# A scan's second try over a chunk: both chunks of a step at once, and the next step's exponents right behind the products

## The chip, the cores and the metric

The kernel runs on one core of a Trainium2 chip. The metric is device time in microseconds for one launch of the whole program (two layers). The engines are named as in the profile: PE is TensorE (matmuls; PEld is its weight load), DVE is VectorE, ACT is ScalarE, POOL is GpSimd, SP is SyncE, which issues most DMAs. PSUM is the matmuls' output memory, eight banks of 512 float32 columns for 128 partitions.

## The reference, cut to what matters

Each layer has three parallel groups of heads: a bidirectional Mamba-2 scan (SSD), windowed attention, and a convolution module. The change touches the scan alone. For each chunk of 128 tokens, each of 16 heads and each direction it computes (cut):

```python
cs = cumsum(da)                                   # inside the chunk
decay = exp(where(tril, cs[l] - cs[s], -inf))     # 128 x 128 per head
cb = einsum('lgn,sgn->gls', c, b)                 # one per group of 8 heads
y_diag = einsum('grls,sgrp->lgrp', cb * decay, x * dt)
states = einsum('lgn,grl,lgrp->grpn', b, exp(cs[-1] - cs), x * dt)
y_off = einsum('lgn,grpn,grl->lgrp', c, entering_state, exp(cs))
y = y_diag + y_off                                # forward and backward, summed
```

There are 1280 tokens, 2 chunks of context and 8 of latents, so 10 chunks. The backward direction has the mirrored mask. The forward and the backward weights of one chunk use the same `cb`, so both directions' `decay * dt` can be added before one product with `x`.

## The kernel before, in words

Each layer runs `ssd_section`, `att_section` and `out_section`, one after the other. `ssd_section` makes the scan's set-up (cumulative sums, logarithms of `dt`, and from both the tiles `L`), then for i = 0 to 3 calls `half(i, xk)` (four heads each), the gemms and taps of one convolution block (`conv_gemm(i)`, `taps()`), and `inputs(i + 1)`, the projections for the next half. `half` stands under `high_priority(AHEAD)`. The order on each engine is not the program's: a planner simulates the program at compile time, starts what is ready by priority, and takes tile slots from each tag's pool as they come free. What it decides is fixed in the program; on the chip each engine runs its instructions in that order.

A half has ten steps `(cf, cb)`: forward chunk `cf` and backward chunk `cb`. Each step multiplies the entering state (`yo`), makes the next state (`stp`, then `S`), and visits both chunks. A chunk is visited twice, once per direction. The first visit starts `yp`, the chunk's sum. The second visit (step 1 and steps 6 to 9; in the last layer steps 6 to 9 alone), called the second try here, adds `yo` and then finishes the chunk:

- `diag(c)` (L872 to L895) builds exponents on PE. The weights operand is `lt`, a tile `L`, with 99 rows used: 48 rows with the high, middle and low bfloat16 part of the negated sums for 16 (direction, head) pairs, 48 for the logarithms, 3 rows of -1. The moving operand is R, whose 96 upper rows select heads and whose rows 96 to 98 hold the chunk's sums, fetched from DRAM (`csd`) by two DMAs on ACT's queue.
- One matmul 128 wide, two of 64, and two that add a mask, go to a PSUM tile `pc`; four of 64, two of them masks, to `pd`. ACT takes the exponential of both (L884, L891), POOL adds the 64 x 64 blocks on the diagonal (L893), and DVE multiplies by `cbs` (L895).
- Two transposes of `yp` (L912) and four products with `xk` (64 wide, two passes each, so x8 in the trace) go to one PSUM tile; ACT copies it to `yT` (L916) and a DMA stores it.

So per half 10 second tries in layer 0 and 8 in layer 1, 72 in all. The tags `ex`, `eb`, `yT` and R have two buffers; the PSUM tag `sm` has four banks (NSM), which all of this, `yo`, `stp` and the transposes of `inputs` share. The gemms use two other banks (`pj`). At each half's start two DVE copies fill both R (L852).

All matmuls but the transposes go through the helper at L96, so they are told apart by tile names. The trace's form `128*64` means 128 rows and 64 columns of weights.

Of the kernel before, what the change touches and what calls it, by code (L numbers as in the profile page):

```python
# [10 lines left out]
F32 = mybir.dt.float32  # L11
# [8 lines left out]
P = 128  # L20
# [39 lines left out]
NSM = 4  # L60
# [7 lines left out]
def build(tc, A, out, stop=None, dbg=None):  # L68
# [26 lines left out]
    def mm(o, l, r, start=True, stop=True):  # L95
        nc.tensor.matmul(o, l, r, start=start, stop=stop)  # L96
# [24 lines left out]
    sel_c = cp.tile([P, 16], BF16, name="sel_c")  # L121
    sel4 = cp.tile([P, 32], F32, name="sel4")
    nc.vector.tensor_reduce(out=sel4[:, 0:16], in_=ident[:, 0:96].rearrange("p (a b) -> p b a", b=16), axis=mybir.AxisListType.X, op=ALU.add)
    nc.vector.tensor_copy(out=sel_c, in_=sel4[:, 0:16])
# [14 lines left out]
    csd = [dp.tile([2, 3, 2, 2, 4, T], BF16, name=f"cs{l}") for l in range(DEPTH)]  # L139
# [401 lines left out]
    def ssd_section(l, last, early):  # L541
        v1 = vec1[l]
        gblocks = LATB if last else ALLB
        with ExitStack() as st:
# [191 lines left out]

            nc.vector.tensor_scalar_mul(out=cs, in0=cs, scalar1=-1.0)
            L = []
            for g in range(2):
                qq = sp.tile([P, NCH, P], BF16, tag=("cbs", "btok")[g], name="qq")  # L740

                def v4(ap):
                    return ap.rearrange("p c (d j) -> p c d j", d=2)

                for c0, t in ((0, cs), (48, ld)):
                    x = v4(v3(t))[:, :, :, 8 * g:8 * g + 8]
                    q = [v4(qq[:, :, c0 + 16 * k:c0 + 16 * k + 16]) for k in range(3)]
                    nc.vector.tensor_copy(out=q[0], in_=x)
                    nc.vector.tensor_tensor(out=x, in0=x, in1=q[0], op=ALU.subtract)
                    nc.vector.tensor_copy(out=q[1], in_=x)  # L750
                    nc.vector.tensor_tensor(out=q[2], in0=x, in1=q[1], op=ALU.subtract)
                nc.gpsimd.memset(qq[:, :, 96:P], -1.0)
                lt = sp.tile([P, T], BF16, tag=f"L{g}", name="L")
                for b0 in range(0, NCH, 4):
                    nb = min(4, NCH - b0)
                    pr = pp.tile([P, 1024], BF16, tag="sm", name="pr", bufs=NSM)
                    for c in range(b0, b0 + nb):
                        nc.tensor.transpose(pr[:, (c - b0) * P:(c - b0 + 1) * P], qq[:, c, :], identb)
# [82 lines left out]
            def half(i, xk):  # L841
# [5 lines left out]
                def sel4(t):  # L847
                    return t.rearrange("p (d h) -> p d h", d=2)[:, :, 4 * hf:4 * hf + 4]
                Rs = []
                for _ in range(2):  # L850
                    R = sp.tile([P, 2, 4, P], BF16, tag="R", name="R", bufs=2)
                    nc.vector.tensor_copy(out=R, in_=sel4(sel_c).unsqueeze(3).to_broadcast([P, 2, 4, P]))  # L852
                    Rs.append(R)
# [11 lines left out]
                nv = [0]  # L865

                def diag(c):

                    R = Rs[nv[0] % 2]
                    nv[0] += 1  # L870
                    for dd in range(2):
                        nc.scalar.dma_start(out=R[96:99, dd], in_=csd[l][g, :, dd, hf, :, c * P:(c + 1) * P])  # L872

                    ll = [lt[0:99, c * P + a:c * P + a + 64] for a in (0, 64)]
                    qs = [slice(0, 64), slice(64, P)]
                    r0, r1 = R[0:99, 0], R[0:99, 1]
                    pc = pp.tile([P, 4, P], F32, tag="sm", name="pc", bufs=NSM)
                    mm(pc[:, :, qs[1]], lt[0:99, c * P:(c + 1) * P], r0[:, :, qs[1]], start=True, stop=False)
                    mm(pc[qs[0], :, qs[0]], ll[0], r0[:, :, qs[0]], start=False, stop=False)
                    mm(pc[qs[1], :, qs[0]], ll[1], r1[:, :, qs[0]], start=False, stop=False)  # L880
                    for q in qs:
                        mm(pc[q, :, q], identb[:, q], mask_lt[:, q].unsqueeze(1).to_broadcast([P, 4, 64]), start=False, stop=True)
                    e = sp.tile([P, 4, P], F32, tag="ex", name="ex", bufs=2)
                    nc.scalar.activation(out=flat(e), in_=flat(pc), func=AF.Exp)  # L884
                    pc = pp.tile([P, 4, P], F32, tag="sm", name="pd", bufs=NSM)[:, :, 0:64]
                    for q, lq in zip(qs, ll):
                        mm(pc[q], lq, r1[:, :, q], start=True, stop=False)
                    for q in qs:
                        mm(pc[q], identb[:, q], mask_gt[:, q].unsqueeze(1).to_broadcast([P, 4, 64]), start=False, stop=True)
                    eb = sp.tile([P, 4, 64], F32, tag="eb", name="eb", bufs=2)  # L890
# [579 lines left out]
```

## Time and profile before

| | us |
|---|---|
| median of 3 runs (2412.1 to 2414.97) | 2413.73 |
| the profiled execution | 2409.47 |
| its span, first to last instruction | 2407.7 |
| PE busy | 2307.0 |
| DVE busy | 1533.2 |
| POOL busy | 1085.7 |
| ACT busy | 979.0 |

The busy time of an engine is the union of its instructions' times. Matmuls are pipelined: each is shown with its whole latency, so they overlap and PE seems busy in gaps shorter than that. The distance between the starts of two matmuls, their pitch, is what one costs. Mean granted clock of TensorE over the span is 0.985 of full speed.

### The profile page before, as it was taken

What the parts mean: (1) busy time and instruction counts of PE and PEld (TensorE: products, weight loads), DVE (VectorE), ACT (ScalarE), POOL (GpSimd) and SP (SyncE); (2) the same over time, 40 slices, a digit from 0 to 9 for tenths busy, and PEclk for the clock granted to TensorE, in tenths of its full rate; (3) what the DMA queues carried; (4) which work ended last, traced back from release to release, by engine and by line L of the source; (5) the groups of instructions that cost most, each with busy time, mean ns of one, the idle gap of its engine ahead of it and who ended that gap; (6) DMA issues with size and microseconds to landing.
All of it is one profiled execution on the core that took longest, in us unless ns stands there. A gap on an engine that the chain in (4) does not pass through costs nothing.

```text
span 2407.7 us, 37133 instructions
## 1 busy us (share of the span) xinstructions
PE 2307.0 (96%) x13453; PEld 1817.5 (75%) x13453; DVE 1533.2 (64%) x2738; ACT 979.0 (41%) x2123; POOL 1085.7 (45%) x1249
## 2 busy tenths in 40 slices
PE   6999999999999999999999999999999999999998
PEld 3787678777877776776888788768768676776798
DVE  4679899941276855865354679979423864865634
ACT  6543243422235454444243443343322355463433
POOL 3237663764453222343233337667575531332333
PEclk8999999999999999999999999999999999999999
DMA  7412212233133112248465311111212312235663
GB/s 225 154 58 87 87 49 64 85 100 111 36 90 105 62 38 70 80 141 264 136 185 168 92 40 45 41 41 43 78 54 62 106 48 67 80 97 171 197 179 107
DMA packets 324248, 237.07 MB, mean 98 GB/s; under 512 B 56066, under 2 KB 280546, under 8 KB 324064
## 3 DMA queue, kind: packets, MB, share of 16 engines
q1 hardware_dynamic: 280832, 193.28, 27.2%
q10 hardware_dynamic: 42336, 41.06, 5.5%
q8 instruction: 106, 1.74, 0.3%
q0 software_dynamic: 896, 0.35, 0.1%
q14 instruction: 78, 0.64, 0.1%
HBM read 181.63 MB, written 53.00 MB: 97 GB/s over the span
## 4 chain that ended last, share of the span: by engine, by line
PE 77%; DVE 9%; DMA 5%; POOL 3%; issue 2%; ACT 2%; SPq 1%; ACTq 0%; DVEq 0%; POOLq 0%
PE pj L96 53%; PE sm L96 6%; PE s L96 4%; PE o L96 3%; PE pt L1086 3%; PE po L96 2%; DVE us L508 2%; DMA raw<-oT 1%; PE pc L96 1%; PE pm L96 1%; DMA wm<-w_mod 1%; POOL ex L893 1%; PE rb L96 1%; DVE acc L596 1%; PE sm L912 1%
## 5 line engine op out<-in xcount | busy, mean ns | idle before, releaser
L96 PE MATMUL pj<-hh,wh 128*128 128x512 f32 (+1 forms) x1840 | 692.7, 377 | 7.8 <-ACT wh L416 2.3
L96 PE MATMUL pj<-hl,wh 128*128 128x512 f32 (+1 forms) x1840 | 686.5, 373 | 1.7 <-POOL hl L199 1.7
L96 PE MATMUL pj<-hh,wl 128*128 128x512 f32 (+1 forms) x1840 | 686.4, 373 | 1.7 <-POOL wl L418 1.6
L418 POOL TENSOR_TENSOR wl<-wr,wh 128x512 fp32r<-128x512 f32 x268 | 362.1, 1354 | 516.8 <-ACT wh L416 482.1
L96 PEld LDWEIGHTS pj<-hh,wh 128*128 128x128 f32 x1840 | 350.0, 190 | 70.7 <-issue 6.8
L96 PEld LDWEIGHTS pj<-hh,wl 128*128 128x128 f32 x1840 | 349.5, 190 | 61.3 <-issue 5.0
L96 PEld LDWEIGHTS pj<-hl,wh 128*128 128x128 f32 x1840 | 350.2, 190 | 59.3 <-issue 5.7
L416 ACT ACTIVATE wh<-wr 128x512 fp32r<-128x512 f32 x344 | 215.6, 630 | 365.5 <-PE pj L96 280.2
L508 DVE SCALAR_TENSOR_TENSOR ua<-gl,vec,ua 128x512 f32<-128x512 f32 (+1 forms) x435 | 303.5, 698 | 12.3 <-ACT ua L506 5.7
L596 DVE SCALAR_TENSOR_TENSOR acc<-raw,vec,acc 128x514 f32<-128x514 f32 (+2 forms) x280 | 191.0, 695 | 21.9 <-ACT acc L593 20.3
L96 PE MATMUL pj<-ho,wh 128*128 128x256 f32 (+1 forms) x896 | 180.3, 300 | 1.0 <-ACT wh L416 1.0
L96 PE MATMUL pj<-hx,wh 128*128 128x512 f32 x512 | 163.7, 400 | 6.9 <-DVE hx L500 2.9
L96 PEld LDWEIGHTS pj<-ho,wh 128*128 128x128 f32 x896 | 145.2, 193 | 6.4 <-ACT wh L416 1.2
L893 POOL TENSOR_TENSOR ex<-ex,eb 64x256 f32<-64x256 f32 x144 | 115.5, 802 | 59.4 <-ACT eb L891 52.4
L933 POOL TENSOR_TENSOR xs<-xk,ws 128x256 f32<-128x256 f32 x144 | 90.7, 641 | 112.0 <-PE sm L96 96.8
L1079 ACT ACTIVATE p<-s,sums 128x512 f32<-128x512 f32 (+1 forms) x144 | 95.5, 663 | 107.7 <-DVE sums L1077 69.4
L1076 DVE TENSOR_REDUCE mx<-s 128x1 f32<-128x512 f32 (+1 forms) x144 | 92.4, 654 | 72.0 <-PE s L96 71.6
L96 PE MATMUL pj<-ho,wl 128*128 128x256 f32 (+1 forms) x448 | 134.6, 301 | 1.1 <-POOL wl L418 0.8
L508 DVE SCALAR_TENSOR_TENSOR us<-gl,vec,us 128x512 f32<-128x512 f32 (+1 forms) x150 | 130.3, 869 | 6.8 <-ACT us L506 4.3
L96 PEld LDWEIGHTS pj<-hx,wh 128*128 128x128 f32 x512 | 97.8, 192 | 30.6 <-DVE hx L500 4.7
L907 POOL TENSOR_TENSOR yp<-yp,ye 128x256 f32<-128x256 f32 x136 | 104.3, 783 | 26.6 <-DVE ye L906 26.1
L1086 PE MATMUL pt<-ident,p 128*128 128x128 f32 x640 | 108.5, 283 | 7.2 <-ACT p L1079 6.5
(325 smaller groups left out, 3951.6 us busy)
## 6 DMA issues: line engine op xcount, KB each, us to landing
wr<-w_in SPq DMA_DIRECT2D x160, 256.0 KB
wr<-w_out SPq DMA_DIRECT2D x114, 256.0 KB
wm<-w_mod SPq DMA_DIRECT2D x64, 256.0 KB
raw<-oT ACTq DMA_DIRECT2D x64, 256.0 KB
wr<-w_out SPq DMA_DIRECT2D x76, 128.0 KB
yT<-yT ACTq DMA_DIRECT2D x72, 128.0 KB
wm<-w_mod SPq DMA_DIRECT2D x16, 512.0 KB
wr<-w_in SPq DMA_DIRECT2D x64, 128.0 KB
```

Of the source, the lines that this page charges most:

```text
L96: nc.tensor.matmul(o, l, r, start=start, stop=stop)
L416: nc.scalar.activation(out=hi, in_=raw, func=AF.Copy)
L418: low_eng[0].tensor_tensor(out=lo, in0=raw, in1=f32(hi), op=ALU.subtract)
L508: nc.vector.scalar_tensor_tensor(out=u if t == 30 else acc, in0=g[:, t:t + n], scalar=vec2[l][:, t, j:j + 1], in1=acc, op0=ALU.mult, op1=A ...
L596: nc.vector.scalar_tensor_tensor(out=acc, in0=raw[:, i0 + t:i0 + t + n], scalar=v1[:, cw:cw + 1], in1=acc, op0=ALU.mult, op1=ALU.add)
L893: nc.gpsimd.tensor_tensor(out=e[q, :, q], in0=e[q, :, q], in1=eb[q], op=ALU.add)
L907: nc.gpsimd.tensor_tensor(out=y, in0=y, in1=ye, op=ALU.add)
L912: nc.tensor.matmul(ps[:, jj * P:(jj + 1) * P], y[:, jj * P:(jj + 1) * P], ident, start=(jj == 0), stop=False, is_transpose=True)
L933: nc.gpsimd.tensor_tensor(out=h3(xs), in0=xc(c), in1=hb(ws3, c, d), op=ALU.mult)
L1076: nc.vector.tensor_reduce(out=mx, in_=s, axis=mybir.AxisListType.X, op=ALU.min)
L1079: nc.scalar.activation(out=flat(p[:, 0:min(nk, 4), :]), in_=s, func=AF.Exp, scale=-1.0, bias=nm[:, j:j + 1], accum_out=sums[:, 3, j:j + 1])
L1086: nc.tensor.transpose(pt[:, q * P:(q + 1) * P], pr[q][:, i, :], ident)
```

## The change

`mm` returns its instruction; `after` makes the instructions traced inside it queue behind a given one on its engine. `diag` and the end of `visit` become `weights(cc)` and `outputs(cc, e)`, each for both chunks of a step. `weights` for the next second try is issued behind the last product of this one; the first is issued at the half's start. `L` now has in its lower 64 rows a 64 x 64 identity (`id64`), and R has masks there, written once per layer, so that the masks come with the same matmul. R has three variants (forward, mixed, backward) of 512 columns. `ex`, `eb` and `yT` hold two chunks and have one buffer each. R's upper rows are filled on ACT at each half's start.

```diff
-    csd = [dp.tile([2, 3, 2, 2, 4, T], BF16, name=f"cs{l}") for l in range(DEPTH)]
+    csd = [dp.tile([2, 3, 2, 3, 4, T], BF16, name=f"cs{l}") for l in range(DEPTH)]
...
+    def after(ins):
+        return tc.issue_after(ins[0].ins) if ins else nullcontext()
...
             for g in range(2):
+                qc = sp.tile([P, NCH, 72], BF16, tag="xk", name="qc", bufs=7)
+                parts(cs, qc, g)
+                for q, c0 in ((slice(0, 64), 24), (slice(64, P), 0)):
+                    nc.scalar.activation(out=qc[q, :, 48:72], in_=qc[q, :, c0:c0 + 24], func=AF.Copy)
...
+                parts(ld, qq, g)
+                nc.gpsimd.memset(qq[:, :, 48:64], -1.0)
+                nc.scalar.activation(out=qq[:, :, 64:P], in_=id64.unsqueeze(1).to_broadcast([P, NCH, 64]), func=AF.Copy)
...
+                        nc.tensor.transpose(pr[0:72, (c - b0) * P:(c - b0 + 1) * P], qc[:, c, :], identb)
+                    cr = sp.tile([72, 512], BF16, tag="xk", name="cr", bufs=7)
+                    nc.scalar.activation(out=cr[:, 0:nb * P], in_=pr[0:72, 0:nb * P], func=AF.Copy)
+                    for v, w in enumerate((0, 2, 1)):
+                        nc.scalar.dma_start(out=csd[l][g][:, :, v].rearrange("a f h t -> (a f) h t")[:, :, b0 * P:(b0 + nb) * P], in_=cr[24 * w:24 * w + 24, 0:nb * P])
...
-                nc.scalar.dma_start(out=csd[l][g].rearrange("a d f h t -> (a d f h) t"), in_=lt[0:48, :])
...
+            Rs = []
+            for _ in range(2):
+                R = sp.tile([P, 3, 4, P], BF16, tag="R", name="R", bufs=2)
+                nc.gpsimd.memset(R[32:64], 0.0)
+                nc.gpsimd.memset(R[64:P, 0:2], 0.0)
+                for v, t0, m in ((0, 0, mask_lt), (1, 64, mask_lt), (2, 0, mask_gt), (2, 64, mask_gt)):
+                    nc.gpsimd.tensor_copy(out=R[64:P, v, :, t0:t0 + 64], in_=m[64:P, 64:P].unsqueeze(1).to_broadcast([64, 4, 64]))
+                Rs.append(R)
...
-                    nc.vector.tensor_copy(out=R, in_=sel4(sel_c).unsqueeze(3).to_broadcast([P, 2, 4, P]))
+                for R in Rs:
+                    for v, d, t0, t1 in ((0, 0, 0, P), (2, 1, 0, P), (1, 1, 0, 64), (1, 0, 64, P)):
+                        nc.scalar.activation(out=R[0:48, v, :, t0:t1], in_=sel_c[0:48, d, 4 * hf:4 * hf + 4].unsqueeze(2).to_broadcast([48, 4, t1 - t0]), func=AF.Copy)
...
+                def weights(cc):
+                    pcs = []
+                    pd = pp.tile([P, 2, 4, 64], F32, tag="sm", name="pd", bufs=NSM)
+                    e = sp.tile([P, 2, 4, P], F32, tag="ex", name="ex")
+                    eb = sp.tile([P, 2, 4, 64], F32, tag="eb", name="eb")
+                    for R, c in zip(Rs, cc):
+                        nc.scalar.dma_start(out=R[48:51], in_=csd[l][g, :, hf, :, :, c * P:(c + 1) * P])
+                    with after(last_mm):
+                        for u, (R, c) in enumerate(zip(Rs, cc)):
+                            ll = [lt[:, c * P + a:c * P + a + 64] for a in (0, 64)]
+                            pc = pp.tile([P, 4, P], F32, tag="sm", name="pc", bufs=NSM)
+                            for v, (q, lq) in enumerate(zip(qs, ll)):
+                                mm(pc[q], lq, R[:, v])
+                            for q, lq in zip(qs, ll):
+                                mm(pd[q, u], lq, R[:, 2, :, q])
+                            pcs.append(pc)
+                    for u in range(2):
+                        nc.scalar.activation(out=flat(e[:, u]), in_=flat(pcs[u]), func=AF.Exp)
+                    nc.scalar.activation(out=eb, in_=pd, func=AF.Exp)
+                    for q in qs:
+                        nc.gpsimd.tensor_tensor(out=e[q, :, :, q], in0=e[q, :, :, q], in1=eb[q], op=ALU.add)
+                    for u, c in enumerate(cc):
+                        nc.vector.tensor_tensor(out=e[:, u], in0=e[:, u], in1=cbs[:, c, :].unsqueeze(1).to_broadcast([P, 4, P]), op=ALU.mult)
+                    return e
...
+                def outputs(cc, e):
+                    ps = sm()
+                    for u, c in enumerate(cc):
+                        for jj in range(2):
+                            nc.tensor.matmul(ps[:, (2 * u + jj) * P:(2 * u + jj + 1) * P], yp[c // 2][:, c % 2, jj * P:(jj + 1) * P], ident, start=(u + jj == 0), stop=False, is_transpose=True)
+                    for u, c in enumerate(cc):
+                        for h in range(4):
+                            k = 2 * u + h // 2
+                            last_mm[:] = [mm(ps[h % 2 * 64:h % 2 * 64 + 64, k * P:(k + 1) * P], xk[c // 2][:, c % 2, h * 64:(h + 1) * 64], e[:, u, h, :], start=False, stop=(u * 2 + h // 2 == 3))]
+                    yT = sp.tile([P, 4, P], F32, tag="yT", name="yT")
+                    nc.scalar.activation(out=flat(yT), in_=ps, func=AF.Copy, scale=0.5)
+                    for u, c in enumerate(cc):
+                        nc.scalar.dma_start(out=yTd[l][:, 2 * i:2 * i + 2, c * P:(c + 1) * P], in_=yT[:, 2 * u:2 * u + 2, :])
...
+                second = ([] if last else [1]) + [6, 7, 8, 9]
+                e = weights(steps[second[0]])
...
+                        if si in second:
+                            outputs((cf, cb), e)
+                            if si < 9:
+                                e = weights(steps[second[second.index(si) + 1]])
```

## Rows read from the trace of the kernel before

**Rows 1.** The page: engine sums (busy us, share, instructions), and the chain by engine.
```profile
PE 2307.0 (96%) x13453; PEld 1817.5 (75%) x13453; DVE 1533.2 (64%) x2738; ACT 979.0 (41%) x2123; POOL 1085.7 (45%) x1249
...
PE 77%; DVE 9%; DMA 5%; POOL 3%; issue 2%; ACT 2%; SPq 1%; ACTq 0%; DVEq 0%; POOLq 0%
```

**Rows 2.** Busy us by stage (a:b, length, then each engine; last clock and DMA).
```profile
core 0: us, PE busy (x) PEld busy (x) DVE busy (x) ACT busy (x) POOL busy (x), PEclk, DMA share, GB/s
...
160.00:500.00 340.00, 331.48 (x2115) 256.07 (x2114) 307.18 (x531) 123.69 (x265) 216.87 (x320) 1.00 0.26 75
500.00:620.00 120.00, 113.34 (x685) 86.43 (x684) 33.78 (x64) 32.59 (x67) 66.59 (x85) 0.97 0.33 93
1400.00:1700.00 300.00, 291.92 (x1645) 232.79 (x1644) 257.40 (x417) 111.30 (x227) 190.69 (x275) 0.99 0.16 42
1700.00:1810.00 110.00, 103.73 (x598) 78.71 (x597) 32.65 (x58) 32.23 (x72) 71.77 (x99) 0.99 0.28 79
...
1560.00:1600.00 40.00, 32.45 (x211) 22.27 (x210) 34.64 (x59) 14.57 (x32) 34.15 (x47) 0.96 0.12 35
```

**Rows 3.** PE in order of time (start, length, instruction): a run of sixteen products.
```profile
346.18 0.39 PE L96 MATMUL pj<-hl,wh 128*128 128x512 f32 x1
346.41 0.39 PE L96 MATMUL pj<-hh,wl 128*128 128x512 f32 x1
346.73 1.09 PE L96 MATMUL sm<-ex,xk 128*64 128x128 f32 x16
347.75 0.50 PE L96 MATMUL pj<-hh,wh 128*128 128x512 f32 x1
348.09 0.40 PE L96 MATMUL pj<-hl,wh 128*128 128x512 f32 x1
```

**Rows 4.** PE in order of time: a run of eight products.
```profile
513.46 0.39 PE L96 MATMUL pj<-hh,wh 128*128 128x512 f32 x1
513.78 0.66 PE L96 MATMUL sm<-ex,xk 128*64 128x128 f32 x8
514.37 0.50 PE L96 MATMUL pj<-hl,wh 128*128 128x512 f32 x1
514.71 0.40 PE L96 MATMUL pj<-hh,wl 128*128 128x512 f32 x1
```

**Rows 5.** PE in order of time: the first exponents.
```profile
175.43 0.51 PE L96 MATMUL pc<-R,L 99*128 99x256 bf16 x3
175.77 0.28 PE L96 MATMUL pc<-mask_lt,identb 128*64 128x256 bf16 x2
175.88 0.28 PE L96 MATMUL pd<-R,L 99*64 99x256 bf16 x2
...
176.20 0.50 PE L96 MATMUL pj<-hl,wh 128*128 128x512 f32 x1
176.54 0.39 PE L96 MATMUL pj<-hh,wl 128*128 128x512 f32 x1
```

**Rows 6.** PE in order of time: the start of the last run.
```profile
1803.72 0.66 PE L96 MATMUL sm<-ex,xk 128*64 128x128 f32 x8 [0.72 <-DVE ex L895]
```

**Rows 7.** Groups by line and form: busy us, mean ns of one, idle before and releasers.
```profile
L758 PE MATMUL pr<-identb,qq 128*128 128x128 bf16 x40 | 3.1, 220 | 0.0
...
L893 POOL TENSOR_TENSOR ex<-ex,eb 64x256 f32<-64x256 f32 x144 | 115.5, 802 | 59.4 <-ACT eb L891 52.4 <-PE pj L96 1.1
L418 POOL TENSOR_TENSOR wl<-wr,wh 128x512 fp32r<-128x512 f32 x268 | 362.1, 1354 | 516.8 <-ACT wh L416 482.1 <-DMA wr<-w_out 11.0 <-DMA xb<-xT 6.9
...
L884 ACT ACTIVATE ex<-pc 128x512 f32<-128x512 f32 x72 | 43.1, 598 | 107.2 <-PE pc L96 40.9 <-PE pd L96 39.9 <-DMA R<-cs 8.1
...
L895 DVE TENSOR_TENSOR ex<-ex,cbs 128x512 f32<-128x512 f32 x72 | 53.9, 749 | 63.6 <-POOL ex L893 63.3
L852 DVE COPY R<-sel_c 128x1024 bf16<-128x1024 bf16 x16 | 14.2, 895 | 3.6 <-PE pd L96 3.4
```

**Rows 8.** DVE in order of time, end of layer 1's last half.
```profile
1796.88 0.69 DVE L895 TENSOR_TENSOR ex<-ex,cbs 128x512 f32<-128x512 f32 x1 [2.78 <-POOL ex L893]
...
1802.98 0.69 DVE L895 TENSOR_TENSOR ex<-ex,cbs 128x512 f32<-128x512 f32 x1 [2.79 <-POOL ex L893]
```

More of the change, by code (lines that the diff above doesn't have):

```diff
@@ L1 @@
-from contextlib import ExitStack
+from contextlib import ExitStack, nullcontext
 from itertools import chain
@@ L95, in mm @@
     def mm(o, l, r, start=True, stop=True):
-        nc.tensor.matmul(o, l, r, start=start, stop=stop)
+        return nc.tensor.matmul(o, l, r, start=start, stop=stop)
+    def after(ins):
+        return tc.issue_after(ins[0].ins) if ins else nullcontext()
     def spread(o, col):
@@ L119, in build @@
     nc.vector.tensor_scalar(out=mask_gt, in0=tril, scalar1=-1.0, scalar2=-NEG, op0=ALU.add, op1=ALU.mult)
-    sel_c = cp.tile([P, 16], BF16, name="sel_c")
+    sel_c = cp.tile([P, 2, 8], BF16, name="sel_c")
     sel4 = cp.tile([P, 32], F32, name="sel4")
-    nc.vector.tensor_reduce(out=sel4[:, 0:16], in_=ident[:, 0:96].rearrange("p (a b) -> p b a", b=16), axis=mybir.AxisListType.X, op=ALU.add)
-    nc.vector.tensor_copy(out=sel_c, in_=sel4[:, 0:16])
+    for d in range(2):
+        nc.vector.tensor_reduce(out=sel4[:, 8 * d:8 * d + 8], in_=ident[:, 24 * d:24 * d + 24].rearrange("p (a b) -> p b a", b=8), axis=mybir.AxisListType.X, op=ALU.add)
+    nc.vector.tensor_copy(out=sel_c, in_=sel4[:, 0:16].rearrange("p (a b) -> p a b", b=8))
+    id64 = cp.tile([P, 64], BF16, name="id64")
+    nc.vector.tensor_tensor(out=id64, in0=identb[:, 0:64], in1=identb[:, 64:P], op=ALU.add)
     nc.vector.tensor_reduce(out=sel4, in_=ident.rearrange("p (a b) -> p b a", b=32), axis=mybir.AxisListType.X, op=ALU.add)
@@ L757, in ssd_section @@
                     for c in range(b0, b0 + nb):
+                        nc.tensor.transpose(pr[0:72, (c - b0) * P:(c - b0 + 1) * P], qc[:, c, :], identb)
[3 more added lines that the diff above has]
+                        nc.scalar.dma_start(out=csd[l][g][:, :, v].rearrange("a f h t -> (a f) h t")[:, :, b0 * P:(b0 + nb) * P], in_=cr[24 * w:24 * w + 24, 0:nb * P])
+                    pr = pp.tile([P, 1024], BF16, tag="sm", name="pr", bufs=NSM)
+                    for c in range(b0, b0 + nb):
                         nc.tensor.transpose(pr[:, (c - b0) * P:(c - b0 + 1) * P], qq[:, c, :], identb)
                     nc.scalar.activation(out=lt[:, b0 * P:(b0 + nb) * P], in_=pr[:, 0:nb * P], func=AF.Copy)
-                nc.scalar.dma_start(out=csd[l][g].rearrange("a d f h t -> (a d f h) t"), in_=lt[0:48, :])
                 L.append(lt)
+            Rs = []
[6 more added lines that the diff above has]
+                Rs.append(R)
             ecs3, ws3, cd3 = v3(ecs), v3(ws), v3(cd)
@@ L864, in half @@
                 yp = {}
[L865 to L880, printed above, removed]
-                    for q in qs:
[L882 to L890, printed above, removed]
-                    nc.scalar.activation(out=eb, in_=pc, func=AF.Exp)
-                    for q in qs:
-                        nc.gpsimd.tensor_tensor(out=e[q, :, q], in0=e[q, :, q], in1=eb[q], op=ALU.add)
-                    ex = [e]
-                    nc.vector.tensor_tensor(out=ex[0], in0=ex[0], in1=cbs[:, c, :].unsqueeze(1).to_broadcast([P, 4, P]), op=ALU.mult)
-                    return ex[0]
```

36 lines of the change are left out of this document (12 added, 24 removed).

## The prediction

> **What bounds the kernel now.** I read the engine sums and the chain of waits first, then the busy time by stage, then TensorE's instructions in order of time around the code that is touched. TensorE (PE) is busy 96% of the span, and 77% of the chain that ended last is its own work [rows 1]. The touched code is `half`, eight calls: in layer 0 between 160 and 620 us, in layer 1 between 1400 and 1810. There PE is busy 331 of 340, 113 of 120, 292 of 300 and 104 of 110 us at full granted clock or nearly so [rows 2]. So PE time taken out there is worth its length as long as PE stays last. The second number to keep is VectorE (DVE): 307 of 340 and 257 of 300 us while halves 0 to 2 of a layer run, but 34 of 120 and 33 of 110 in the last half, which has no convolution taps beside it [rows 2]. ScalarE (ACT) is at 36% and GpSimd (POOL) at 64% of those stretches and can take some more.
>
> Busy time hides what the change is about, since matmuls overlap. The start times show it. In plain gemm work a matmul of 512 columns starts every 0.23 us (346.18 to 346.41). A run of sixteen products of form 128*64 takes, from 346.41 to the second gemm matmul behind it at 348.09, 1.68 us; without the two gemm pitches that is 1.22 [rows 3]. A run of eight takes 513.46 to 514.71, 1.25 less 0.46, so 0.79 [rows 4]. Eight more products cost 0.43 us, so a run that stands alone pays 0.36 us for getting in and out of form 128*64: the first matmul starts 0.32 instead of 0.23 after its predecessor, and the second gemm matmul behind the run 0.34 instead of 0.23. A run of exponents: 175.43 to 176.54, 1.11 us, less one gemm pitch 0.88; in it are one matmul 128 wide and four pairs (the two of a pair, one for each half of the partitions, start together), each with 0.11 us of pitch, 0.55, so 0.33 us are the switches [rows 5]. Between 175 and 1806 us there are 159 runs of form 128*64 in the two sections, 93 in layer 0 and 66 in layer 1, for 72 second tries (the first is that of [rows 5], the last that of [rows 6]): over two per try, since products and exponents stand apart and `pc` and `pd` are often parted too.
>
> **The change part by part.** *Columns of the exponents.* Before, a chunk costs five pitches of 0.11 us. After, it is one pair of 512 columns (twice 0.11, from the pitch for 256) and one pair of 256: 0.33. The masks come in through the weights' lower 64 rows instead of four matmuls. 0.22 x 72 = -15.8 us of PE.
>
> *Runs.* After, one run per step if the next step's exponents stand right behind this step's products, and one more at each half's start: 36 + 8 = 44 runs. If other work gets between them, 36 + 36 = 72. At 0.345 us (mean of 0.36 and 0.33) the first gives 115 x 0.345 = -39.7, the second 87 x 0.345 = -30.0. I take 50 runs, -37.6 us, near the first: the exponents need only R, whose transfer has a whole step's time, and three free banks.
>
> By the Trainium skill, "TensorEngine Tiling (Array Packing)", section "Instruction Overhead", each matmul carries about 60 cycles of overhead, by which 360 fewer matmuls would give back, as an estimate from that page, 9 us more at 2.4 GHz. The trace disagrees: pairs of 256 columns follow each other at 0.11 us [rows 5], half the 0.23 us of 512 columns [rows 3], so the columns are paid and I add nothing.
>
> *Set-up on PE.* 40 more transposes; today's 40 take 3.1 us [rows 7], and the new ones are no larger: +3.1. **PE in all: -15.8 - 37.6 + 3.1 = -50.3 us**, 0.70 per second try: 7.0 for each half of layer 0 (10 tries), 5.6 for each of layer 1 (8).
>
> *DVE.* The 16 copies that fill R go (14.2 us, 0.895 each), the products of `e` with `cbs` stay 72 of the same size [rows 7]. R is filled by 64 ACT copies instead, of 256 or 512 elements on 48 partitions. No row shows that operand, so I price it between nothing and the 0.60 us of an exponential over 512 [rows 7], up to 38 us on an engine that is two thirds idle. They come before a half's first state step and can only wait for the exponents of the half before, which are issued a step before its end. Cost on the path 0; without that cover up to 8 x 0.60 = 4.8 us a half.
>
> *POOL.* 144 additions of 64x256 at 0.80 become 72 of 64x512. The nearest row of 512 elements is the 1.35 us of `wl`, so 97 against 115 us [rows 7]; at worst twice 0.80, no change. The zeroing and masks of R, once per layer, are some 3600 elements for each of the two tiles: at the pace of `wl` at most 19 us per layer, of constants alone, so they can run anywhere ahead of half 0, beside the gemms of the section's start. The exponents of `pd` merge, as do the copies `yT`: less ACT time, not on the path.
>
> *Transfers.* `csd` is written in 18 pieces per layer instead of 2, and R read in one piece per chunk instead of two. The write delays only half 0's start; PE has a convolution's gemms beside it. I take +1.5 us for the whole set-up of both layers, between nothing and one step of 6.1 us [rows 8] in which half 0 would start late.
>
> *The wait that the change adds.* `e`, `eb` and `yT` are single now, and exponents stand behind the products on PE's queue. From one step's exponents to the next step's: three exponentials at 0.60 and two additions at 1.35 [rows 7], two DVE products at 0.69 [rows 8], sixteen PE products 0.86 (twice 0.43), exponents of two chunks 0.66: 1.8 + 2.7 + 1.4 + 0.9 + 0.7 = 7.5 us, about 8.5 with the hand-overs. Now, at the end of layer 1's last half where nothing else is left for PE, a step takes 1796.88 to 1802.98, 6.1 us [rows 8]. So the chain of a half is up to 2.4 us longer per step over three steps (the first of the four finds its `e` made in advance). While gemms remain, PE fills the wait and it costs nothing; queued behind the waiting products are the next state's matmuls, whose engine users (DVE, POOL) have other work.
>
> *Banks.* The exponents take three of the four `sm` banks until ACT has read them, 1.8 us; `yo` and the state product of the next step wait that long. Hidden by gemms on the `pj` banks likewise.
>
> **What of it arrives.** Halves 0 to 2 of layer 0: 3 x 7.0 = 21. DVE would then have some 302 us of work in 319, 95%, and some of its order no longer fits beside PE: I take three quarters, -16. Halves 0 to 2 of layer 1: 3 x 5.6 = 16.8, but between 1560 and 1600 PE is busy 32 of 40 us and waits for the chain [rows 2], so half a half is lost (14), and with DVE at 86% I take 0.85 of it: -12. Layer 0's last half, partly waiting: half of 7.0, -3.5. Layer 1's last half ends on the chain: 0. With set-up: -16 - 12 - 3.5 + 1.5 = **-30 us**. The profiled execution took 2409.47 us (span 2407.7), so 2379.5; the median of the runs shown is 2413.73, 4.3 above it, so **2384 us**.
>
> **The rivals.** *All of PE's gain arrives* (DVE keeps up, no tail): -50.3 with 44 to 50 runs and the chain hidden: 2364 to 2366. For it: PE's share of the chain; against: DVE at 90% and the tails. *The runs don't form* (banks or the order keep products and exponents apart, split further as `pc` and `pd` are now): columns -15.8, set-up +4.6, a few switches less, and half of that lost as above: -8 to -14, about 2402. For it: the order of work is planned ahead and split these blocks before; against: the ordering edge and the merged blocks. *Slower: the single `e`.* If gemms beside a half run out before its last steps, every one of the 24 step-to-step waits shows its 2.4 us: 7.2 per half, 58 in all, against -50.3: +8, 2421. It decides from 6.3 us per half on (50.3 / 8). For it: 1560 to 1600 and layer 1's tail, where that already happens; against: PE fully busy in the other halves.
>
> **How the numbers follow.** Forecast (2374 to 2395) 0.50, all of the gain 0.18, runs don't form 0.17, slower 0.15. No change is within 0.2%, 4.8 us, what a measurement of this kernel can tell. The forecast gives 0.49 faster and 0.01 same; the second all faster; the third 0.11 faster, 0.05 same, 0.01 slower; the fourth 0.03 same, 0.12 slower. Faster 0.78, same 0.09, slower 0.13. The range is 2364 to 2412: its low end is the full gain, and the upper end leaves out most of the slower case.
>
> **What would show it.** Right: about 50 runs of form 128*64 in the two sections, products and exponents in one timeline stretch without 128*128 between; 360 matmuls fewer into `pc` and `pd`; DVE's share in halves 0 to 2 at 94% or more; ACT busier by up to 40 us. Wrong: over 72 such runs; PE idle before `sm<-ex,xk` with DVE `ex` as releaser in halves 0 to 2; halves that follow each other no sooner than now.

## The result, and the profile after

The changed kernel takes 2437.68 us, median of 4 runs (2437.35 to 2438.63), beside 2414.35 for the kernel before in the same comparison: ratio 1.0099, 95% interval 1.0084 to 1.0114. It is slower by 1%; forecast were 2384 us and a gain. The profiled execution took 2437.36 us with a span of 2435.7, 28 more than the profiled one of before; that one lay 5 us below the median of its runs, so of the 28 some 23 are the change's.

The page of the kernel after, engine sums (busy us, share, instructions), answers to [rows 1]:

```profile
PE 2282.7 (94%) x13133; PEld 1819.8 (75%) x13133; DVE 1540.6 (63%) x2726; ACT 1002.4 (41%) x2139; POOL 1087.3 (45%) x1201
```

PE has 320 matmuls fewer (360 gone, 40 transposes more) and 24 us less busy time, and yet the span is longer. The stages of the kernel after, in the stretches of [rows 2] and one more (length, then busy us of each engine; the last three columns are granted clock, DMA share, GB/s):

```profile
core 0: us, PE busy (x) PEld busy (x) DVE busy (x) ACT busy (x) POOL busy (x), PEclk, DMA share, GB/s
160.00:500.00 340.00, 310.59 (x1927) 251.36 (x1924) 301.83 (x512) 126.75 (x255) 201.71 (x274) 0.96 0.24 71
500.00:620.00 120.00, 115.23 (x696) 90.30 (x697) 40.83 (x74) 32.15 (x67) 74.64 (x93) 0.99 0.37 108
1400.00:1700.00 300.00, 274.03 (x1469) 224.40 (x1468) 247.46 (x399) 114.50 (x228) 173.65 (x243) 0.97 0.15 40
1700.00:1810.00 110.00, 103.29 (x565) 83.57 (x565) 42.31 (x67) 31.03 (x62) 71.87 (x91) 0.99 0.25 69
1560.00:1600.00 40.00, 28.65 (x143) 21.84 (x141) 37.98 (x65) 8.54 (x15) 28.83 (x40) 0.91 0.08 21
1800.00:1835.00 35.00, 21.60 (x124) 13.94 (x124) 10.28 (x17) 7.55 (x15) 18.65 (x20) 0.72 0.18 55
```

PE was idle 8.5 us in 160 to 500 and 8.1 in 1400 to 1700 before; now 29.4 and 26.0, and the granted clock there is 0.96 and 0.97 where it was 1.00 and 0.99. At the end of layer 1's section, 1800 to 1835, PE is busy 21.6 of 35 us at 0.72. So I divide the span of the profiled execution, window by window of 20 us, into three parts: busy time multiplied by the granted clock is work at the full 2.4 GHz, the rest of the busy time is the loss to the lower clock, and what is left is idle. It is an estimate, since busy time holds the latency of the matmuls. "Runs" are runs of form 128*64 with exponents or products of a second try, both sections (159 before, as the prediction counted).

```
(us)                        work  lower clock  idle   span   runs
before                     2278.3    28.7     100.7  2407.7  159
after                      2234.6    48.2     153.0  2435.7   55
difference                  -43.7   +19.5     +52.3   +28.0
```

TensorE's work fell by 44 us, near the 50 of the forecast, in 55 runs, near the forecast's 50. Idle time and clock gave back 72.

Where? The same instructions of both traces tell: the attention's transposes `pt` that follow a layer's scan, and the last `rcols` transposes ahead of layer 1's scan. Each row shows the first and the last start; the first two rows are the kernel before.

```profile
L1015 PE MATMUL pt<-ident,vt x20: 270/272/273, 614.8 to 1835.3; 128*128 128x128 f32 x20
L100 PE MATMUL sm<-ident,rcols x8: 271/272/273, 79.9 to 1348.6; 128*128 128x128 f32 x8
...
L1051 PE MATMUL pt<-ident,vt x20: 270/272/328, 621.0 to 1864.6; 128*128 128x128 f32 x20
L104 PE MATMUL sm<-ident,rcols x8: 271/272/273, 78.4 to 1350.2; 128*128 128x128 f32 x8
```

Behind layer 0's scan the kernel after is 6 us late (5 at the last of that layer's `pt`), ahead of layer 1's scan 1.6 us, behind it 29. So almost the whole loss arises in layer 1: from the last `rcols` to the last `pt`, work fell there by 16 us and idle time and clock gave back 44; in layer 0, from 140 us to its last `pt`, work fell by 26.5 and they gave back 32. (These are single executions. Another one of nearly the kernel before, that with many writes below, took 5 us more than the kernel before in the stretch of layer 0 and 8 more in that of layer 1, with the same median; the changed kernel took 5 and 28 more.)

What PE waited for in these two stretches, kernel before (layer 1; none in layer 0), then kernel after, layer 0 and layer 1 (us in total, times, longest; each wait is put down to the releaser that came last):

```profile
PE sm L912 <- POOL yp L907: 3.1, 4, 0.9
...
PE sm L939 <- POOL yp L932: 8.6, 7, 4.9
...
PE sm L939 <- POOL yp L932: 23.5, 16, 6.1
```

So 29 of the 52 us of new idle time are waits of a step's transposes for `yp`. Another 10 are waits in the set-up for the copies of `qc`, `cr` and `L`. Two places show how. First the set-up of layer 1, kernel after, ACT and its queue in order of time (start, length, instruction; in brackets the idle time before it and its releaser):

```profile
1413.16 0.74 ACTq L778 DMA_DIRECT2D cs<-cr  x1
...
1414.68 2.94 ACTq L778 DMA_DIRECT2D cs<-cr  x4
1417.66 0.60 ACT L782 ACTIVATE L<-pr 128x512 bf16<-128x512 bf16 x1 [3.08 <-DMA cs<-cr]
...
1421.83 0.82 ACT L764 ACTIVATE qc<-qc 64x240 bf16<-64x240 bf16 x2 [1.97 <-DMA cs<-cr]
...
1432.18 0.60 ACT L782 ACTIVATE L<-pr 128x512 bf16<-128x512 bf16 x1 [2.48 <-DMA cs<-cr]
...
1433.21 0.60 ACT L845 ACTIVATE btok<-sm 128x512 f32<-128x512 f32 x1
```

The same place of the kernel before:

```profile
1413.74 0.32 ACTq L760 DMA_DIRECT2D cs<-L  x1
...
1414.50 1.10 ACT L814 ACTIVATE btok<-sm 128x512 f32<-128x512 f32 x2
```

Each of the 18 writes holds ACT's queue for some 0.74 us where each of the 2 held it 0.32, and copies of `L`, `qc` and `btok` wait behind them. `btok`, an operand of half 0's first state product, comes 19 us later, and that product starts at 1448.65 instead of 1430.06. In layer 0 it starts at 179.5 instead of 167.2.

Then the steps. Kernel after, PE and POOL at the end of layer 0's second half, in order of time:

```profile
348.49 0.40 PE L96 MATMUL pj<-hh,wl 128*128 128x512 f32 x1
...
349.04 1.09 PE L96 MATMUL sm<-ex,xk 128*64 128x128 f32 x16
349.96 0.39 PE L96 MATMUL pc<-R,L 128*64 128x512 bf16 x2
...
354.24 2.94 POOL L918 TENSOR_TENSOR ex<-ex,eb 64x512 f32<-64x512 f32 x2
...
358.17 1.97 PE L96 MATMUL sm<-ex,xk 128*64 128x128 f32 x16 [3.38 <-DVE ex L920]
359.92 0.64 PE L96 MATMUL pc<-R,L 128*64 128x512 bf16 x2
...
363.48 2.59 POOL L918 TENSOR_TENSOR ex<-ex,eb 64x512 f32<-64x512 f32 x2 [6.30 <-ACT eb L916]
366.14 2.41 POOL L932 TENSOR_TENSOR yp<-yp,ye 128x256 f32<-128x256 f32 x2
367.47 0.69 PE L939 MATMUL sm<-ident,yp 128*128 128x128 f32 x2 [4.89 <-POOL yp L932]
...
375.20 0.50 PE L96 MATMUL pj<-hh,wh 128*128 128x512 f32 x1 [1.66 <-ACT raw L595]
```

Products and exponents do stand in one run, at 349.04 with nothing of form 128*128 between. But between 348.49 and 375.20 no gemm starts: a chain without cover, in the middle of the section. (Layer 0 as a whole made up for most of this, as shown above; layer 1 did not.) And POOL takes the next step's additions of `eb` into `e` (L918) before this step's `yp` (L932), for which the transposes wait. The last step of layer 1 shows all of it, kernel after:

```profile
1820.44 1.97 PE L96 MATMUL sm<-ex,xk 128*64 128x128 f32 x16
1822.20 0.64 PE L96 MATMUL pc<-R,L 128*64 128x512 bf16 x2
...
1823.63 2.08 PE L96 MATMUL sm<-S,ct 128*128 128x256 f32 x4
...
1824.54 0.59 ACT L916 ACTIVATE eb<-pd 128x512 f32<-128x512 f32 x1
1825.21 2.59 POOL L918 TENSOR_TENSOR ex<-ex,eb 64x512 f32<-64x512 f32 x2 [5.44 <-ACT eb L916]
1825.81 0.76 DVE L931 TENSOR_TENSOR ye<-sm,ecs 128x256 f32<-128x256 f32 x2 [6.62 <-PE sm L96]
...
1827.84 1.82 DVE L920 TENSOR_TENSOR ex<-ex,cbs 128x512 f32<-128x512 f32 x2 [1.27 <-POOL ex L918]
1827.88 2.36 POOL L932 TENSOR_TENSOR yp<-yp,ye 128x256 f32<-128x256 f32 x2
...
1830.30 0.69 PE L939 MATMUL sm<-ident,yp 128*128 128x128 f32 x2 [0.56 <-POOL yp L932]
1830.91 1.98 PE L96 MATMUL sm<-ex,xk 128*64 128x128 f32 x16
```

From products to products 10.47 us, 6.1 before [rows 8]: products 1.76, exponents 1.43, exponentials until POOL starts 1.58, additions 2.67, `yp` 2.42, transposes 0.61. `ye` was there at 1826.57; `yp` waited 1.3 us for POOL. The products take 1.97 where [rows 3] shows sixteen in 1.09, and `pc` and `pd` start 0.43 apart instead of 0.22 at 349.96: PE runs near the lower of its two clock levels (1.2 of 2.4 GHz). The granted clock is 0.61 in 1820 to 1835, after 0.81 in 1800 to 1820, where PE was busy 12.2 of 20 us.

The kernel after, groups by line (busy us, mean ns of one, idle before), answer to [rows 7]:

```profile
L932 POOL TENSOR_TENSOR yp<-yp,ye 128x256 f32<-128x256 f32 x136 | 109.4, 823 | 31.7 <-DVE ye L931 31.1
L918 POOL TENSOR_TENSOR ex<-ex,eb 64x512 f32<-64x512 f32 x72 | 92.3, 1282 | 97.1 <-ACT eb L916 94.4
L920 DVE TENSOR_TENSOR ex<-ex,cbs 128x512 f32<-128x512 f32 x72 | 66.9, 970 | 41.2 <-POOL ex L918 41.1
...
L880 ACT ACTIVATE R<-sel_c 48x512 bf16<-48x512 bf16 x32 | 18.8, 622 | 1.3 <-POOL R L788 1.3
...
L880 ACT ACTIVATE R<-sel_c 48x256 bf16<-48x256 bf16 x32 | 12.0, 409 | 0.0
```

### The profile page after: what moved, and what is told of

It reads as the page before. It is cut to its first block, busy times and chain, and to the rows that moved or that the text cites. A ratio compares the mean times of both kernels' runs of the same rounds, so it can differ in the third digit from the quotient of the medians.

```text
span 2435.7 us, 36265 instructions
## 1 busy us (share of the span) xinstructions
PE 2282.7 (94%) x13133; PEld 1819.8 (75%) x13133; DVE 1540.6 (63%) x2726; ACT 1002.4 (41%) x2139; POOL 1087.3 (45%) x1201
## 3 DMA queue, kind: packets, MB, share of 16 engines
q1 hardware_dynamic: 280832, 193.28, 26.5%
## 5 line engine op out<-in xcount | busy, mean ns | idle before, releaser
L96 PE MATMUL pj<-hh,wh 128*128 128x512 f32 (+1 forms) x1840 | 691.7, 376 | 10.4 <-ACT raw L595 4.9
L918 POOL TENSOR_TENSOR ex<-ex,eb 64x512 f32<-64x512 f32 x72 | 92.3, 1282 | 97.1 <-ACT eb L916 94.4
L932 POOL TENSOR_TENSOR yp<-yp,ye 128x256 f32<-128x256 f32 x136 | 109.4, 823 | 31.7 <-DVE ye L931 31.1
```

Of the source, the lines that this page charges most:

```text
L96: return nc.tensor.matmul(o, l, r, start=start, stop=stop)
L918: nc.gpsimd.tensor_tensor(out=e[q, :, :, q], in0=e[q, :, :, q], in1=eb[q], op=ALU.add)
L932: nc.gpsimd.tensor_tensor(out=y, in0=y, in1=ye, op=ALU.add)
```

## The experiments

Theory S put the loss on the late set-up, C on the chain with its single `e` and the edge that ties exponents to outputs. After the first four, theory W joined S with POOL's order. "The edge" is the ordering that `after` sets. Times are medians; the intervals are of the ratio to the kernel before in the same comparison (its medians: 2414.4 to 2416.0, so a difference between variants of two comparisons carries some 2 us more). The planner orders every variant anew, so an edit also moves work that it doesn't name (moving the additions alone takes the kernel before from 159 runs to 146); no run here holds that order fixed.

**Writes on SP** (`cr` of a group in the slot of `ex`):

```diff
-                    cr = sp.tile([72, 512], BF16, tag="xk", name="cr", bufs=7)
+                cr = sp.tile([72, T], BF16, tag="ex", name="cr")
...
-                        nc.scalar.dma_start(out=csd[l][g][:, :, v]...[:, :, b0 * P:(b0 + nb) * P], in_=cr[24 * w:24 * w + 24, 0:nb * P])
+                    nc.sync.dma_start(out=csd[l][g][:, :, v]..., in_=cr[24 * w:24 * w + 24, :])
```

> The changed kernel with one part of the set-up altered: the sums go to DRAM in 3 pieces per group of heads instead of 9, issued on SP's queue instead of ACT's, from a tile of its own instead of one of the xk slots. Theory S (set-up): in the changed kernel each of the 18 pieces per layer holds ACT's queue for about 0.73 us and the group's second half waits behind them, so half 0 starts 12 us (layer 0) and 18 us (layer 1) later than before and never gets it back; here the start comes at least 8 us earlier in each layer and the time falls by 12 to 22 us, to 2416 to 2426. Theory C (chain): the steps of a half, not its start, are what is longer; the time stays at 2437 within 5.

2430.79 us, 1.0059 (1.004 to 1.0079), 7 below the change: outside S's range and outside C's. The trace says why it is short of S's: one slot for both groups made a new wait for the write. ACT of this variant, set-up of layer 1:

```profile
1421.95 1.08 ACT L776 ACTIVATE cr<-pr 72x512 bf16<-72x512 bf16 x2 [3.71 <-DMA cs<-cr]
```

**The kernel before with many writes:**

```diff
-                nc.scalar.dma_start(out=csd[l][g]..., in_=lt[0:48, :])
+                    for a in range(3):
+                        nc.scalar.dma_start(out=csd[l][g, a]...[:, b0 * P:(b0 + nb) * P], in_=lt[16 * a:16 * a + 16, b0 * P:(b0 + nb) * P])
```

> The kernel before with one part of the change alone: its write of the sums to DRAM, one piece per group on ACT's queue, is cut into 9 pieces per group (3 row groups for each of 3 column blocks), issued right behind each block's copy as the change does. Theory S: the start of half 0 comes later by the issue time of 16 more pieces, 6 to 12 us per layer, and the time rises by 6 to 15 us over the kernel before. Theory C: no change within 4 us.

2416.15 us, 0.9999 (0.9986 to 1.0013): no change, as C said. So the number of writes alone isn't it. Here a write of 16 rows holds ACT some 0.44 us, not 0.74. ACT's copies still wait for them, 13.4 us over both layers against 18.7 in the change, but half 0 starts only 2.9 and 5.4 us later than before, against 12.3 and 18.6; a start that much later cost nothing that the runs could tell. The longest wait in layer 1:

```profile
1418.38 0.87 ACT L759 ACTIVATE L<-pr 128x512 bf16<-128x512 bf16 x2 [5.05 <-DMA cs<-L]
```

**No edge** (exponents may be issued ahead of the outputs):

```diff
-        return tc.issue_after(ins[0].ins) if ins else nullcontext()
+        return nullcontext()
```

> The changed kernel without the ordering edge that puts the next step's exponents behind the last product; everything else, the single e too, stays. Theory C, if the edge is what makes the chain long: exponents are issued up to 1.4 us earlier in a step whose gemms have run out, the steps at the end of layer 1 fall from 10.4 to about 9 us, and the time falls by 4 to 12 us; if it is the single e and POOL's order, no change within 4. Theory S: no change within 4 us, 2433 to 2441.

2423.43 us, 1.0041 (1.0026 to 1.0055), 14 below the changed kernel, more than C's 4 to 12, with 85 runs instead of 55: the edge saves 30 runs and costs more. The last steps of layer 1, from one `yT` to the next, take 8.8 us in the mean instead of 10.4, and PE's waits for `yp` in layer 1's scan fall from 23.5 to 15.4.

**By chunk** (new products, R and set-up; two `e`, `eb` and `yT`, no edge):

```diff
-                    e = sp.tile([P, 2, 4, P], F32, tag="ex", name="ex")
+                    e = sp.tile([P, 1, 4, P], F32, tag="ex", name="ex", bufs=2)
...
-                            outputs((cf, cb), e)
+                            outputs((c,), weights((c,)))
```

> The changed kernel with its new products, L, R and set-up, but chunk by chunk as before: exponents and products of one chunk at its visit, e, eb and yT of one chunk with two buffers, no ordering edge. Theory C: the step at the end of layer 1's last half goes back from 10.4 to 6 to 7 us and the time falls by 8 to 20 us, to 2417 to 2429, what remains over the kernel before being the set-up. Theory S: half 0 still starts 12 and 18 us late, the time stays above 2430.

2439.06 us, 1.0102 (1.0087 to 1.0117): as slow as the change, as S said. It doesn't clear the single `e`, though, because it gives back the runs too. It has 141 of them and 27.5 us more work than the change, with 24 us less idle time (sums below); PE's waits for `yp` in layer 1 fall from 23.5 to 5.9. So the long chain does cost, about what the merged runs save. Two `e`, the step of one chunk, the missing edge and the exponents made no step ahead come together here, and the run does not part them.

**Writes on SP from own slots:**

```diff
+                crs = [sp.tile([72, T], BF16, tag="ex", name="cr")] if g == 0 else [sp.tile([72, 1024], BF16, tag="eb", name="cr"), sp.tile([72, 256], BF16, tag="yT", name="cr")]
...
+                        nc.sync.dma_start(out=csd[l][g][:, :, v]...[:, :, t0:t0 + n], in_=cr[24 * w:24 * w + 24, :])
```

> The changed kernel whose summed parts go to memory in nine writes on SP's queue instead of eighteen on ACT's, each group from slots of its own, so that no copy waits for a write (in the earlier variant with the writes on SP the second group's copy of `cr` waited 3.7 us for the first group's write). Only the set-up is touched; the edge and POOL's adds stay. Theory W (the products give back what was forecast, and the time goes to idle of PE and to its lower clock, in a late set-up and in a chain in which `yp` stands behind the adds of exponents on POOL): `btok` of layer 1 comes some 10 us earlier than in the changed kernel (1433 us), 2420 to 2428. Rival H (a late set-up costs nothing, because the gemms beside it are only used earlier): no better than the earlier variant, 2429 to 2437.

2420.57 us, 1.002 (1.001 to 1.003): 17 less than the change, in W's range. From start to end of the same stretches as above, 15 of it are layer 1's, where half 0 starts 13 us earlier than in the change, and 7 layer 0's, where it starts no earlier (179.8); so the late start is not all that the writes cost. (The rest of the profiled execution is 6 longer than the change's.) ACT of this variant in the same set-up, its last copy of `L` and the first of `btok`, 11 us earlier than in the change:

```profile
1418.20 0.38 ACT L781 ACTIVATE L<-pr 128x256 bf16<-128x256 bf16 x1
...
1422.47 1.36 ACT L850 ACTIVATE btok<-sm 128x512 f32<-128x512 f32 x3 [2.01 <-PE sm L849]
```

**Additions of `eb` on DVE:**

```diff
-                        nc.gpsimd.tensor_tensor(out=e[q, :, :, q], in0=e[q, :, :, q], in1=eb[q], op=ALU.add)
+                        nc.vector.tensor_tensor(out=e[q, :, :, q], in0=e[q, :, :, q], in1=eb[q], op=ALU.add)
```

> The changed kernel with the 72 adds of `eb` into `e` on DVE instead of POOL (1282 ns each on POOL; DVE does its products of the same 512 columns in 0.75 to 0.91 us). Set-up and edge stay. Theory W: the next step's `yp` adds no longer stand behind 2.6 us of adds, the step at the end of a half goes from 10.4 us to about 8, and the waits named POOL yp (3.5 us in 340 to 380, 5.75 us in 1500 to 1520, and those at 1580 and 1800) go: 2422 to 2431. Rival M (the single `e` makes the step long whoever adds: products, exponents, adds and outputs follow one another): 2434 to 2442, DVE being fuller by some 50 us.

2422.80 us, 1.0026 (1.0012 to 1.004), 15 less, as W said. The last steps of layer 1 take 8.9 us in the mean instead of 10.4, and PE's waits for `yp` in layer 1 fall from 23.5 to 15.8. W had them go; they do not, the edge and the single `e` being still there.

**All three:** own slots, additions on DVE, no edge.

> The changed kernel with all three: writes on SP from slots of their own, the adds of `eb` on DVE, and no edge that holds the next step's exponents behind this step's outputs. Theory W: the three add up, -10 to -15 for the set-up, -8 to -14 for the adds, -14 for the edge as measured: 2398 to 2413, faster than before. Rival M: the edge's 14 and a few for the set-up are all there is, 2416 to 2425.

2408.56 us, 0.9972 (0.9961 to 0.9983): 0.3% faster than the kernel before, in W's range. It is 29 below the change, where the three single gains add to 46. PE's waits for `yp` in layer 1 are down to 8.4 us.

**By chunk with both mends** (writes on SP, additions on DVE):

> New products, new R and new set-up chunk by chunk (two `e`, no edge; 2439 as measured), now with the writes on SP from slots that are not waited for and the adds of `eb` on DVE. Its runs of the form 128*64 stay as many as before (some 160), so its work on PE is only the columns below the kernel before. Theory W: 2415 to 2424, since the late set-up and POOL are mended but no switch is saved. Rival N (filling R, its DMAs and the 0.2 us more of each exponent cost what is missing, whatever the set-up does): 2431 to 2440.

2413.10 us, 0.9996 (0.9988 to 1.0005): on W's side, 2 us below its range, and 26 below the same by chunk. It has 139 runs, and its work at full clock is 15.4 us below the kernel before.

**Writes and additions, edge kept:**

> The changed kernel with the writes on SP from slots of their own and the adds of `eb` on DVE; the edge stays, so that exponents stand right behind outputs: some 50 runs of the form 128*64 in the two sections, where the kernel without the edge has 88. Theory W with the edge harmless by itself (its 14 us came of the late set-up and of POOL): 35 runs fewer by 0.345 us each are 12 us of PE, and the time is 2396 to 2406, below the 2408.6 without the edge. Rival E (the edge itself costs: it holds the exponents back until the outputs are through, and the step at the end of a half stays at 8.9 us, where it is 7.9 without it): 2411 to 2420.

2429.93 us, 1.0068 (1.0054 to 1.0081): a miss for both, 24 us above W's range and 10 above E's, and 9 worse than the writes alone. It has 53 runs and 7 us less work than all three mended, but 15 us more idle time and 8.5 more at the lower clock. On DVE the additions can stand ahead of `ye` now, as on POOL they stood ahead of `yp`. This variant, near the end of layer 1:

```profile
1797.81 0.59 ACT L921 ACTIVATE eb<-pd 128x512 f32<-128x512 f32 x1
1798.43 1.39 DVE L923 TENSOR_TENSOR ex<-ex,eb 64x512 f32<-64x512 f32 x2 [8.77 <-ACT eb L921]
...
1799.85 0.76 DVE L936 TENSOR_TENSOR ye<-sm,ecs 128x256 f32<-128x256 f32 x2
```

The `yo` of that `ye` began at 1797.72 and took 1.02; `ye` lost 1.1 us. The variant with the additions alone has that order too (1811.68 ahead of 1813.10), so it doesn't explain the difference; why the two mends together are worse than either with the edge stays open.

**The kernel before, its additions on DVE** (a control):

```diff
-                        nc.gpsimd.tensor_tensor(out=e[q, :, q], in0=e[q, :, q], in1=eb[q], op=ALU.add)
+                        nc.vector.tensor_tensor(out=e[q, :, q], in0=e[q, :, q], in1=eb[q], op=ALU.add)
```

> The kernel before with its own adds of `eb` (160 of 64x256) on DVE instead of POOL, as a control for what moving them did to the changed kernel (-15). Theory W (what cost was that the changed kernel's adds of 1282 ns, four columns halves at a time, stand ahead of the next step's `yp`; before, the adds of one chunk stand just ahead of its own product, behind its `yp`): -4 to +6, 2410 to 2421. Rival P (POOL's adds are slow in any kernel and DVE's are better, nothing of the change): -10 or more, below 2405.

2406.86 us, 0.9965 (0.9952 to 0.9978), between the two theories: 8 us of the 15 are to be had without the change. Groups of this variant (802 ns on POOL in [rows 7]; the additions are 144, not the 160 of the expectation):

```profile
L893 DVE TENSOR_TENSOR ex<-ex,eb 64x256 f32<-64x256 f32 x144 | 72.8, 506 | 36.1 <-ACT eb L891 34.9
```

**All three, additions divided between DVE and POOL:**

```diff
-                    for q in qs:
-                        nc.gpsimd.tensor_tensor(out=e[q, :, :, q], ...)
+                    for eng, q in zip((nc.vector, nc.gpsimd), qs):
+                        eng.tensor_tensor(out=e[q, :, :, q], ...)
```

> The variant with all three mended (2408.6), its adds of `eb` divided: the lower half of each pair on DVE, the upper on POOL, side by side. Theory W: the adds take 1.3 us beside each other instead of 2 x 0.83 us on DVE, but `yp` stands behind one of 1.28 us on POOL again: 2404 to 2412. Rival V (DVE's queue is what the step now waits for: S and the products stand behind the adds): below 2404.

2403.05 us, 0.9954 (0.994 to 0.9968), the fastest of all, just on V's side; its interval reaches into W's range, so it doesn't decide between them. Against the kernel before with its own additions on DVE, in the same comparison, it is 4 us less and the intervals overlap.

**Writes from own slots and no edge:**

> The changed kernel with the writes on SP from slots of their own and no edge; the adds of `eb` stay on POOL, whole. It closes the table of edge, writes and adds: with the edge, the writes alone gave 17 us and the adds on DVE 15, but both together 2429.9, 9 above the writes alone. Theory E (the edge is what keeps the mends from adding up: without it, exponents no longer wait for outputs, so what the set-up gives is kept): the edge's 14 and the set-up's 17 add up, 2402 to 2410, and the adds' place is worth little then. Rival A (mends never add up, because each frees the same idle time of PE): 2414 to 2422, and only DVE's adds bring the 2408.6 and the split ones the 2403.1.

2417.24 us, 1.0006 (0.9995 to 1.0017): A. Without the edge the writes give 6 us (8 by the ratios) instead of 17, and the additions on DVE then 9 more. By the sums below each mend alone takes 14 to 15 us of idle time from the change and all three together 32, not 44: in part they remove the same idle time.

Sums over windows of 20 us again:

```
(us)                               work  lower clock  idle   runs
writes on SP                     2235.0    54.6     138.5    54
before, many writes              2275.7    38.1     104.8  151
by chunk                         2262.1    44.8     129.2  141
no edge                          2242.4    45.4     137.7   85
own slots                        2237.9    43.2     138.3   50
additions on DVE                 2235.3    48.3     138.8   54
own slots + additions on DVE     2238.0    52.2     136.2   53
own slots, no edge               2238.5    48.3     129.0   85
all three                        2245.3    43.7     121.4   88
all three, additions divided     2240.6    41.6     122.2   82
by chunk with both mends         2262.9    35.3     113.2  139
before, additions on DVE         2273.8    27.7     102.7  146
```

Each row is one execution. That of the kernel before with many writes lies 4 us above the median of its runs, that of the kernel before 4 below; the medians do not differ, and yet the column of the lower clock differs by 9 us. So a difference of less than some 10 us in that column says nothing by itself. The drop from the kernel before to the changed one is borne out by all runs, though: the mean granted clock lies between 0.980 and 0.987 in the 80 executions of the kernel before, and between 0.973 and 0.977 in the four of the changed kernel.

## Why the prediction was wrong

*Columns, runs, transposes: right.* Work at full clock fell by 43.7 us, forecast -50.3; with the 104 runs that really went (159 to 55) the forecast's own prices give -15.8 - 35.9 + 3.1 = -48.6. The rival "the runs don't form" is out. (By the same prices the rival "all of PE's gain" would be 2361 with 44 runs, not 2364; nothing hangs on it.) Of the signs of being wrong, PE idle before `sm<-ex,xk` with DVE `ex` as releaser did show (3.38 us at 358.17), and DVE's share in halves 0 to 2 of layer 0 was 89%, not the 94% of the signs of being right.

*"While gemms remain, PE fills the wait and it costs nothing": the main failure.* PE waited 32.1 us for `yp` in the two sections, 3.1 before. Its order puts no gemm between 348.49 and 375.20, in a half that was thought covered. The rival of the single `e` named this condition and the side of the result (2421; it came to 2438). But its price (2.4 us a step) missed what decides: the step is 10.47 us long, not 8.5. Of this 2.42 us are `yp`, which my chain left out because I moved additions from one size to another without asking who stands behind them on POOL; 1.7 us are products and exponents (3.19 instead of 0.86 + 0.66): at 349.04 the same run took 1.79, so 1.4 of it is the lower clock and 0.3 the switches. The DVE products that I did count, 1.4, run beside `yp`. How much of the chain is the single `e`, how much the edge and how much POOL's order is parted only in this: leaving out the edge alone gives 14 us, and taking the additions off POOL 15 (8 of them also without the change). The run by chunk shows that shorter steps take the waits away, not that the single `e` made them.

*"I take +1.5 us for the whole set-up of both layers": mis-sized.* The bound was one step of 6.1 us; half 0 started 12.3 us late in layer 0 and 18.6 in layer 1, and with the writes on SP from own slots the kernel is 17 us faster with the edge, 6 without. I had counted the 18 writes as a delay of half 0 only, not as an occupation of ACT's queue with copies behind them. In layer 0 half 0 stays 12.6 us late without them; what makes it so was not taken apart.

*The lower clock: a missing term.* +19.5 us in the two profiled executions. No gap of PE was priced at more than its length.

*POOL's size and ACT's: right, their order not.* Additions 92.3 us (forecast 97) and fills of R 30.8 (up to 38). "Cost on the path 0" for R was not taken apart by a run; at 360.68 one such copy stands ahead of the exponentials of the step above, and at 361.68 two stand between the first and the second.

*"What of it arrives: -30":* nothing arrived. The factors (three quarters, 0.85) came of DVE's share; in the kernel after DVE is busy 302 of 340 us with PE idle beside it, and the longest waits of PE there are for POOL's `yp`.

What stays of the change when its three costs are mended is small: 2403.05 against 2406.86 for the kernel before with its own additions on DVE, not told apart. The additions divided were not tried in the kernel before. The mended kernel still has 33 us less work than that one, and 20 us more idle time and 14 more at the lower clock.

## What to carry to other kernels

Price an edit in three columns: work taken from the engine that bounds, new idle time, and what the granted clock loses behind that idle time; here the first was right to 7 us and the others, left at nothing, undid it. Look at each stage by itself: layer 0 nearly broke even, layer 1 did not. For every instruction that is moved earlier or made larger, list what stands behind it on its queue (`yp` behind the additions, copies behind DMA issues), also where that engine's share is under 50%. A stretch is covered by gemms only if the order of instructions shows gemms in it: look at the start times there, not at the mean share.

## What the runs showed of the hardware

A DMA issue on ACT's queue took 0.32 us for the 48-row `cs<-L`, about 0.44 for pieces of 16 rows, and 0.71 to 0.74 for pieces of 24 rows that go out by three indices, whether of 512 columns or of 256 (three in 2.22 at 1419.56). Behind four such pieces ACT's next copy waited 3.08 us.

DVE and POOL are both slower when their operations on these tiles run side by side. A DVE product takes 0.69 us alone [rows 8] and 0.91 beside `yp` (1827.84, two in 1.82), and a `yp` on POOL 0.74 where no product runs (353.55 in the kernel after) and 1.18 beside the products (1827.88, two in 2.36). Divided side by side, the addition of `eb` takes 1588 ns on POOL, where it takes 1282 in the change. The groups of the variant with the additions divided:

```profile
L923 POOL TENSOR_TENSOR ex<-ex,eb 64x512 f32<-64x512 f32 x36 | 57.2, 1588 | 74.2 <-ACT eb L921 49.2 <-ACT ex L920 17.6 <-PE sm L96 5.1
L923 DVE TENSOR_TENSOR ex<-ex,eb 64x512 f32<-64x512 f32 x36 | 32.1, 891 | 58.1 <-ACT eb L921 51.0 <-ACT ex L920 7.0
```

The Trainium skill, "SBUF — State Buffer", section "Who interferes with whom", has the rule: a DVE instruction with two inputs in SBUF contends with a GpSimd instruction that reads SBUF, through a shared port pair that is an exclusive lock. These times agree in direction; no run here shows whether one waits in full.
